# Layer 0 of a two-layer encoder: the attention gate's modulation row summed on TensorE, a different cut of the input projection, and reshaped LayerNorm chains

## The chip, the core and the metric

The kernel runs on one core of a Trainium2 chip. It is given the device time in microseconds (us), the median of three runs. The engines named below are TensorE (PE, with its weight loads shown as PEld), VectorE (DVE), ScalarE (ACT), GpSimd (POOL) and SyncE (SP), which issues all the transfers of this kernel on one queue. TensorE accumulates in PSUM; the other data lie in SBUF. All weights are float32 in HBM, and each is read once.

## The reference, cut to what matters

One sequence of 256 tokens with 2048 features goes through two layers. The modulation of a layer is a product of one row, the SiLU of the condition `c`, with a matrix of 2048 x 12288; it is cut into six parts of 2048 numbers each (shift, scale and gate of the attention block, then of the feed-forward block).

```python
cond = jax.nn.silu(c)
for l in range(DEPTH):
    mod = cond @ w_ada[l] + b_ada[l]
    sh1, sc1, g1, sh2, sc2, g2 = [m[:, None, :] for m in jnp.split(mod, 6, axis=-1)]
    u = x * (1.0 + sc1) + sh1
    proj = u @ w_in[l]
    ...            # three attention groups, their outputs RMS-normalised and joined to y
    x = layer_norm(DEEPNORM_ALPHA * x + (1.0 + g1) * (y @ w_o[l]), ln1_g[l], ln1_b[l])
    u = x * (1.0 + sc2) + sh2
    gu = u @ w_gu[l]
    h = jax.nn.silu(gu[..., :D_FF]) * gu[..., D_FF:]
    x = layer_norm(DEEPNORM_ALPHA * x + (1.0 + g2) * (h @ w_down[l]), ln2_g[l], ln2_b[l])
return x
```

## The kernel before, in words

Activations are held with features on the 128 partitions and the 256 tokens along the free axis; a row of 2048 features is 16 such tiles, numbered k on the input side and n on the output side of a product. Weights arrive as 1 MB transfers of 128 x 2048 (`wload`, L238 to L262). Most are split in two halves of 1024 columns into a rounded part `hi` (ACT, L254) and a rest `lo` (DVE, L255), so that a float32 product is made of three fast matmuls of 256 columns: hi times the rounded input, hi times the input's rest, lo times the rounded input. In `gemm_t` (L283) the first two are one matmul of 512 columns; `mm_one` (L308) issues them as three lines, L310 to L312. Nine of the sixteen `w_o` tiles of layer 0 are not split but multiplied in full float32 (`wload_f32`, `gemm_f32`, L279); a float32 matmul shows in the trace as two instructions.

All 1 MB loads of split weights and of the modulation matrix share four buffers, the tag `raw`. A load is issued by SP when the fourth load before it has been used up, and SP issues in program order.

**Modulation.** `ada` (L199) loads one block of 128 modulation columns (1 MB) and sums it against the condition in one DVE instruction (L207, `ada<-ada,cond,vec`). The order is a list, `ada_pending`: for each k the scale and shift of layer 0 (parts 1 and 0), then the sixteen blocks of its gate (part 2), then parts 4 and 3, and so on. `pace` takes blocks from this list at a fixed number per us of planned work; `need` forces those that are wanted next.

**Layer 0, front.** `first_x` (L433) makes input tile X[k] when its two modulation sums are there. The 14 tiles in `RES` accumulate in PSUM while X arrives, one k at a time (`rows`, `in_r` in the trace). The nine tiles in `ROT` use one PSUM bank in turn (`in_rot`): from k = 8 on, each gets its first 8 k values in one go while X arrives (`first_half`), and its last 8 later, as a filler between attention heads (`w_in_tile`, `in`). `_stream0` (L55) writes the weights in that order.

**Attention.** `weave` (L764) runs a group's heads with a list of fillers, one ahead of each head, and up to three pieces of other work around the group's RMS normalisation (`normed`). The groups are a (4 heads), b (6) and c (6). The value projections `va` and `vc`, the query and key expansions `qn`, `qp`, `kn`, the values `vb` and, in group c, the first ten k values of seven `w_o` tiles (`oh`) are such pieces. In `rms_bcast` (L351) the inverse norms of the tokens are put on a diagonal by two DVE instructions and spread over the partitions by a matmul with ones.

**LayerNorm.** `residual` (L567) adds an output tile into `ax` and keeps two running sums over the tiles, s1 of the values and s2 of the squares (L582, L583). After the last tile, `ln_and_next` (L462) reduces both over the partitions (`token_stat`, `lnst`), works out mean and inverse deviation on columns of two, puts the four columns on diagonals (DVE L481, ACT L483), spreads them by two matmuls (`lnbr`, `lnbn`) and makes the next X tiles. `spin` puts idle matmuls between, so that TensorE does not stand still. The split of the next stage's first weights is held back until the residual of tile KT - 3 = 13 is done (`lastr`, `gates`). L999 has a one-element Sqrt (`warm`) ahead of the third tile of the last feed-forward product.

## Time and profile before

| | us |
|---|---|
| three runs | 2296.77, 2297.22, 2301.22 |
| median | 2297.22 |
| the profiled execution, own time | 2295.78 |
| its span, first to last instruction | 2294.0 |
| TensorE busy in it | 2211.5 (96%) |
| VectorE busy in it | 1732.6 (76%) |
| ScalarE busy in it | 1224.9 (53%) |

The profiled execution is 1.4 us below the median of the runs. Busy time of TensorE is modelled and includes overlap of neighbouring matmuls, so 96% does not say that it ran at its peak; shares over the whole span mix stages with different limits, and the rows further below are therefore taken by stage. The rows of windows name the engines by their place: PE, PEld, DVE, ACT, POOL. In layer 0 the stages follow the program: X arrives until 162 us, the attention groups run until 370 us, the remaining `w_o` tiles until 432.6 us, the first LayerNorm until 439 us, and the feed-forward block until 1181 us; its LayerNorm ends at 1194 us, and layer 1 ends the span.

### The profile page before, as it was taken

To read this page: it belongs to the slowest core of one execution; us is meant where nothing else is said; L and a number is where in the kernel's file an instruction comes from. 1 tells how busy PE (TensorE), PEld (TensorE's weight loads), DVE (VectorE), ACT (ScalarE), POOL (GpSimd) and SP (SyncE) were. 2 spreads that over 40 slices of the span, in tenths; PEclk is the share of its full clock that TensorE was granted. 3 is DMA by queue.
4 is the path that set the end of the run, shared out by engine and by line. 5 is a ranking of instruction groups with operands and counts; after the bars stand their busy time and mean duration, and the time that the engine had idled before them with its cause. 6 is when DMAs were issued, how large, how long until landed. Compare 5 with 4: busy or idle time off the path is not lost.

```text
span 2294.0 us, 33731 instructions
## 1 busy us (share of the span) xinstructions
PE 2211.5 (96%) x13074; PEld 1964.7 (86%) x13074; DVE 1732.6 (76%) x2444; ACT 1224.9 (53%) x2038; POOL 207.2 (9%) x175
## 2 busy tenths in 40 slices
PE   6888999999999999999999999999999999999997
PEld 5787988898888888888878898878888888888886
DVE  6778998688888888898888576788666665566566
ACT  3337672464555455445557566557455545545555
POOL 0000020000000310110230000330000020011014
PEclk9999999999999999999999999999999999999999
DMA  9997899568998798799755554456577566546542
GB/s 355 354 363 289 324 333 366 209 246 303 323 329 328 281 361 335 256 354 338 286 192 215 201 217 165 155 194 236 195 249 265 213 222 228 186 164 212 195 157 105
DMA packets 89730, 590.64 MB, mean 257 GB/s; under 512 B 10081, under 2 KB 10209, under 8 KB 31329
## 3 DMA queue, kind: packets, MB, share of 16 engines
q1 hardware_dynamic: 89570, 588.49, 70.1%
q8 instruction: 102, 1.67, 0.3%
q14 instruction: 58, 0.48, 0.1%
HBM read 586.35 MB, written 2.10 MB: 257 GB/s over the span
## 4 chain that ended last, share of the span: by engine, by line
PE 87%; DVE 7%; ACT 3%; issue 2%; POOL 1%; DMA 0%; ACTq 0%; DVEq 0%
PE gu L288 25%; PE gu L290 13%; PE dn L288 13%; PE dn L290 7%; PE in L288 3%; PE o L279 3%; DVE ada L207 3%; DVE lo L255 2%; PE in L290 1%; ACT hi L254 1%; PE oh L605 1%; PE gu_h L605 1%; PE in L605 1%; PE in_r L310 1%; PE gu L312 1%
## 5 line engine op out<-in xcount | busy, mean ns | idle before, releaser
L255 DVE TENSOR_TENSOR lo<-raw,hi 128x1024 fp32r<-128x1024 f32 (+2 forms) x790 | 878.4, 1139 | 317.2 <-issue 149.2
L254 ACT ACTIVATE hi<-raw 128x1024 fp32r<-128x1024 f32 (+2 forms) x790 | 758.9, 968 | 460.8 <-PE gu L288 193.1
L288 PE MATMUL gu<-X,hi 128*128 128x512 f32 x2528 | 603.1, 391 | 0.0
L288 PEld LDWEIGHTS gu<-X,hi 128*128 128x128 f32 x2528 | 465.1, 188 | 89.5
L207 DVE CUSTOM_DVE_ANT_0 ada<-ada,cond,vec 128x2048 f32<-128x2048 f32 x192 | 450.0, 2351 | 30.0 <-DMA ada<-in_w_ada 20.7
L288 PE MATMUL dn<-H,hi 128*128 128x512 f32 x1386 | 339.7, 392 | 0.2 <-DVE H L337 0.2
L290 PEld LDWEIGHTS gu<-X,lo 128*128 128x128 f32 x2528 | 324.2, 191 | 12.3
L290 PE MATMUL gu<-X,lo 128*128 128x256 f32 x2528 | 328.0, 283 | 0.0
L288 PEld LDWEIGHTS dn<-H,hi 128*128 128x128 f32 x1386 | 252.6, 189 | 49.6 <-DVE H L337 3.0
L290 PEld LDWEIGHTS dn<-H,lo 128*128 128x128 f32 x1386 | 183.1, 191 | 9.9 <-DVE lo L255 0.3
L290 PE MATMUL dn<-H,lo 128*128 128x256 f32 x1386 | 186.5, 283 | 0.1
L332 POOL TENSOR_TENSOR mix<-mix,cma 128x256 f32<-128x256 f32 x64 | 80.7, 1261 | 1148.7 <-ACT cma L331 1116.3
L324 ACT ACTIVATE cmb<-gu 128x256 f32<-128x256 f32 x158 | 60.5, 383 | 114.8 <-PE gu L290 114.7
L310 PE MATMUL in_r<-X,hi 128*128 128x256 f32 x224 | 66.7, 319 | 37.1 <-ACT X L336 34.8
L310 PEld LDWEIGHTS in_r<-X,hi 128*128 128x128 f32 x224 | 47.2, 220 | 41.6 <-ACT X L336 39.0
L983 ACT ACTIVATE gu<-gu 128x256 f32<-128x256 f32 x82 | 34.1, 417 | 81.6 <-DVE gu L327 81.6
L897 POOL TENSOR_SCALAR nbc<-cs 128x384 f32<-128x384 f32 x12 | 24.4, 2030 | 566.6 <-DVE mn_c L397 255.2
L337 DVE TENSOR_TENSOR H<-gu,H 128x256 fp32r<-128x256 f32 x82 | 34.6, 423 | 48.6 <-ACT H L336 48.6
L311 PE MATMUL in_r<-X,hi 128*128 128x256 f32 x224 | 69.4, 315 | 0.1
L288 PE MATMUL in<-X,hi 128*128 128x512 f32 x272 | 69.5, 402 | 0.0
L327 DVE SCALAR_TENSOR_TENSOR gu<-gu,cmb 128x256 f32<-128x256 f32 x158 | 66.3, 419 | 1.0 <-ACT cmb L324 0.4
L312 PE MATMUL in_r<-X,lo 128*128 128x256 f32 x224 | 66.4, 309 | 0.4 <-DVE lo L255 0.4
(385 smaller groups left out, 3043.0 us busy)
## 6 DMA issues: line engine op xcount, KB each, us to landing
ada<-in_w_ada SPq DMA_DIRECT2D x192, 1024.0 KB, 5.4
raw<-in_w_gu SPq DMA_DIRECT2D x176, 1024.0 KB, 5.2
raw<-in_w_dn SPq DMA_DIRECT2D x128, 704.0 KB, 4.1
raw<-in_w_in SPq DMA_DIRECT2D x46, 1024.0 KB, 5.3
raw<-in_w_o SPq DMA_DIRECT2D x23, 1024.0 KB, 4.8
wf<-in_w_o SPq DMA_DIRECT2D x18, 512.0 KB, 10.3
raw<-in_w_va SPq DMA_DIRECT2D x8, 1024.0 KB, 4.8
raw<-in_w_uq SPq DMA_DIRECT2D x6, 1024.0 KB, 4.9
```

What stands on the lines that cost most here:

```text
L207: ve.tensor_tensor_reduce(out=w, in0=w, in1=cond, op0=ALU.mult, op1=ALU.add, scale=1.0, scalar=vcol(l, V_ADA + part * KT + k), accum_out=m ...
L254: ac.activation(out=hi[:, :n], in_=raw[:, c0:c0 + n], func=AF.Copy)
L255: eng.tensor_tensor(out=lo[:, :n], in0=raw[:, c0:c0 + n], in1=hi[:, :n].bitcast(F32), op=ALU.subtract)
L279: m_ = pe.matmul(acc[:, :S], lhsT=w[i // 8][:, i % 8 * P:(i % 8 + 1) * P], rhs=X[k][:], start=(i == 0), stop=(i == len(kts) - 1))
L288: pe.matmul(acc[:], lhsT=get(c0 + i * P, P)[0], rhs=X[kts[i]][:], start=(i == 0), stop=False)
L290: last_mm[0] = raw_ins(pe.matmul(acc[:, :S], lhsT=get(c0 + i * P, P)[1], rhs=X[kts[i]][:, :S], start=False, stop=(i == n - 1)))
L310: m_ = pe.matmul(acc[:, :S], lhsT=h, rhs=x[:, :S], start=first, stop=False, **kw)
L311: pe.matmul(acc[:, :S], lhsT=h, rhs=x[:, S:], start=False, stop=False, **kw)
L312: last_mm[0] = raw_ins(pe.matmul(acc[:, :S], lhsT=lo, rhs=x[:, :S], start=False, stop=end, **kw))
L327: ve.scalar_tensor_tensor(out=dst, in0=acc[:, :S], scalar=scale, in1=t, op0=ALU.mult, op1=ALU.add)
L332: po.tensor_tensor(out=dst, in0=dst, in1=t, op=ALU.add)
L605: pe.matmul(acc[:], lhsT=h, rhs=x[:], start=first, stop=False)
```

## The change

**Gate on TensorE.** The sixteen gate blocks of layer 0 (part 2, `PE_ADA`) are no longer summed by DVE. `ada_pe` loads a block of the matrix in the other orientation (input features on the partitions) and runs 16 float32 matmuls over it, each with one column of the condition repeated over 32 columns as weights and 128 columns of the block as moving data. Matmul i writes the PSUM strip of 32 partitions that begins at 32 * (i % 4) (`tile_position`), so four partial sums are left. ACT copies them out (128 x 128), and at the next load `fold_rows` adds the four strips with one matmul against a column `sel` that has a one at every 32nd partition; ACT adds the bias.

**Input tiles.** The nine `ROT` tiles go to k = 12 while X arrives, in two pieces of 6 k values, at the places that `_rows` lists; the last 4 follow as fillers. The fillers of layer 0's groups a and b are dealt out anew.

**`w_o` tiles.** Of the nine float32 tiles of layer 0, the even ones (8, 10, 12, 14) are split and multiplied by `gemm_one`.

**LayerNorm.** The sums of tiles 0 to 14 are reduced by `ln_sums` ahead of the last four k values of tile 15's product; tile 15's own values and squares are reduced straight from `ax` and the square, without going through s1 and s2. The diagonals are gone: each column is repeated over 128 columns as weights of a matmul with the identity, here and in `rms_bcast`. Of the idle matmuls, the first six go, six become four, and seven become five. Tile 14's additions move from POOL to DVE, and the next stage's first splits wait for tile 14 in place of 13. The one-element Sqrt is tied to the last SiLU.

```diff
+KP = 6
+def _rows():
+    todo = [(j, c) for c in range(2) for j in range(len(ROT))]
+    per = {6: 2, 7: 2, 8: 2, 9: 2, 10: 1, 12: 2, 13: 2, 14: 2, 15: 3}
+    return [(k, [todo.pop(0) for _ in range(per.get(k, 0))]) for k in range(KT)]
...
+PE_ADA = ((0, 2),)
...
+            if (l, part) in PE_ADA:
+                ada_pe(l, part, k)
+                continue
...
+    def ada_pe(l, part, k):
+        fold_rows()
+        w = wp.tile([P, D], F32, tag="raw", bufs=RAWB, name=f"adap{l}_{part}_{k}")
+        sy.dma_start(out=w, in_=w_adag[PE_ADA.index((l, part)), k])
+        acc = pg(f"arow{l}_{part}_{k}")
+        first = None
+        for i in range(KT):
+            j = 32 * (i % 4)
+            with after(first):
+                m_ = pe.matmul(acc[j:j + 32, :P], lhsT=condT[:, i:i + 1].to_broadcast([P, 32]),
+                               rhs=w[:, i * P:(i + 1) * P], start=(i < 4), stop=(i >= KT - 4), tile_position=(0, j))
+            first = first or raw_ins(m_)
+        r = sb.tile([P, P], F32, tag="arow", bufs=2, name=f"arsb{l}_{part}_{k}")
+        ac.activation(out=r, in_=acc[:, :P], func=AF.Copy)
+        folds.append((l, part, k, acc, r))
+
+    def fold_rows():
+        while folds:
+            l, part, k, acc, r = folds.pop(0)
+            pe.matmul(acc[:, S:S + 1], lhsT=r[:], rhs=sel, start=True, stop=True)
+            ac.activation(out=mods[l, part][:, k:k + 1], in_=acc[:, S:S + 1], func=AF.Identity,
+                          bias=vcol(l, V_ADA + part * KT + k), scale=1.0)
...
-        dg = tmp(f"dg_{name}", "dg", 2)
-        for h in range(2):
-            ve.tensor_scalar(out=dg[:, h * P:(h + 1) * P], in0=ident, scalar1=r[:, h:h + 1], scalar2=None,
-                             op0=ALU.mult)
...
-        pe.matmul(bc[:, :S], lhsT=ones, rhs=dg[:], start=True, stop=True)
+        for h in range(2):
+            pe.matmul(bc[:, h * P:(h + 1) * P], lhsT=r[:, h:h + 1].to_broadcast([P, P]), rhs=ident, start=True, stop=True)
...
-        st = pa("y", 1, f"lnst{l}_{which}")
-        spin(f"a{l}_{which}", 6)
-        token_stat([s1, s2], inv[2048], [0, 2], st)
-        spin(f"b{l}_{which}", 6)
+        ln_sums(l, which, [(ax[:, KT - 1], last_sq)], False, True)
+        st = stat[0]
+        spin(f"b{l}_{which}", 4)
...
-            if i < 2:
-                ve.tensor_scalar(out=d_, in0=ident, scalar1=m[:, i:i + 1], scalar2=None, op0=ALU.mult)
-            else:
-                ac.activation(out=d_, in_=ident, func=AF.Copy, scale=m[:, i:i + 1])
...
+            last_mm[0] = raw_ins(pe.matmul((bcr if i < 2 else bcn)[:, i % 2 * P:(i % 2 + 1) * P],
+                                           lhsT=m[:, i:i + 1].to_broadcast([P, P]), rhs=ident, start=True, stop=True))
...
-            po.tensor_tensor(out=ax[:, n], in0=ax[:, n], in1=t, op=ALU.add)
+            (ve if final and n == KT - 2 else po).tensor_tensor(out=ax[:, n], in0=ax[:, n], in1=t, op=ALU.add)
...
+                if n == KT - 1:
+                    return q
...
-                if l == 0:
-                    gemm_f32(acc, wload_f32(w_o[l, n]), Yf, allk)
+                if l == 0 and n % 2:
+                    gemm_f32(acc, wload_f32(w_o[l, n]), Yf, allk, sums_in if n == KT - 1 else None)
...
+                    if l == 0:
+                        gemm_one(acc, get, 0, Y, allk)
...
-            if n == KT - 3:
+            if n == KT - 2:
                 lastr = r_
...
-                    ac.activation(out=warm, in_=eps_ln, func=AF.Sqrt)
+                    with after(silu[0]):
+                        ac.activation(out=warm, in_=eps_ln, func=AF.Sqrt)
```

What this does to the order of the instructions is shown at three places. The first is PE in layer 0, behind the last `in_rot` matmuls. `st_kv` is the first RMS sum, `in_22` the filler tile 22, `va` the value projection of group a, and in the names of the changed kernel `adap` is a gate block, `arow` its strips and `arsb` their copy. Before, tile 22 has 24 matmuls left there (three of them are shown), then the projection begins:

```order
L344 MATMUL st_kv_1493<-inv_109,sqk_139 128x1 x2
L310 MATMUL in_22_8_1466<-X_8_699,hi_1_1404 128x256
L311 MATMUL in_22_8_1466<-X_8_699,hi_1_1404 128x256
L312 MATMUL in_22_8_1466<-X_8_699,lo_1_1405 128x256
...
L428 MATMUL s_a_0_1701<-ka_0_119,qa_0_115 128x256 x2
L428 MATMUL s_a_1_1784<-ka_1_120,qa_1_116 128x256
L669 MATMUL va_0_1502<-hi_0_1509,X_0_160 128x512
L669 MATMUL va_1_1503<-hi_0_1509,X_0_160 128x512
```

In the changed kernel the same place reads:

```order
L362 MATMUL in_22_12_1627<-X_15_1451,hi_1_1552 128x256
L363 MATMUL in_22_12_1627<-X_15_1451,hi_1_1552 128x256
L364 MATMUL in_22_12_1627<-X_15_1451,lo_1_1553 128x256
L396 MATMUL st_kv_1642<-inv_112,sqk_142 128x1 x2
L252 MATMUL arow_2_0_1527<-cs,arsb_2_0_1544 128x1
L241 MATMUL arow_2_1_1654<-adap_2_1_1652,condT 32x128 x16
L730 MATMUL va_0_1648<-hi_0_1675,X_0_163 128x512
L730 MATMUL va_1_1649<-hi_0_1675,X_0_163 128x512
```

Tile 22 is finished ahead of `st_kv` with 12 matmuls, and a gate block's fold and the next block's 16 matmuls stand ahead of the projection; thirteen of the sixteen gate blocks stand on PE between X[15] and the first scores of group b, six of them (1 to 6) from here to the end of `va`.

The second place is SP's queue behind the last modulation pair of X, before:

```order
L205 DMA ada_1_15_1344<-in_w_ada 128x2048
L205 DMA ada_0_15_1348<-in_w_ada 128x2048
L246 DMA raw_1398<-in_w_in 128x2048
L155 DMA cs<-in_consts 128x1024
L156 DMA snk<-in_sink 128x12
L752 DMA nba_123<-in_rpb 128x1536
L205 DMA ada_2_0_1504<-in_w_ada 128x2048
L246 DMA raw_1507<-in_w_va 128x2048
```

and in the changed kernel:

```order
L294 DMA raw_1394<-in_w_in 128x2048
L221 DMA ada_1_15_1442<-in_w_ada 128x2048
L221 DMA ada_0_15_1446<-in_w_ada 128x2048
L294 DMA raw_1466<-in_w_in 128x2048
L235 DMA adap_2_0_1525<-in_w_adag 128x2048
L294 DMA raw_1546<-in_w_in 128x2048
L167 DMA cs<-in_consts 128x1025
L168 DMA snk<-in_sink 128x12
```

One more `w_in` load stands ahead of the pair (19 in place of 18), and two `w_in` loads with the first gate block between them stand behind it, where one was.

The third place is DVE at the end of layer 0's feed-forward block, before:

```order
L574 SCALAR_TENSOR_TENSOR ax<-dn_3_13_11149,mod_5_100,ax 128x256
L583 TENSOR_TENSOR s_0_2_10590<-s_0_2_10590,rq_dn_3_13_11176 128x256
L255 TENSOR_TENSOR lo_0_11353<-raw_11350,hi_0_11352 128x1024
L255 TENSOR_TENSOR lo_1_11357<-raw_11350,hi_1_11356 128x1024
L574 SCALAR_TENSOR_TENSOR ax<-dn_3_14_11190,mod_5_100,ax 128x256
L583 TENSOR_TENSOR s_0_2_10590<-s_0_2_10590,rq_dn_3_14_11217 128x256
L569 SCALAR_TENSOR_TENSOR ax<-dn_3_15_11231,mod_5_100,ax 128x256
L582 TENSOR_TENSOR s_0_2_10589<-s_0_2_10589,ax 128x256
L583 TENSOR_TENSOR s_0_2_10590<-s_0_2_10590,rq_dn_3_15_11266 128x256
L470 TENSOR_TENSOR lnm_2_11289<-lnst_2_11270,lnm_2_11289 128x2
```

and in the changed kernel:

```order
L632 TENSOR_TENSOR ax<-ax,rt_dn_3_14_11675 128x256
L633 SCALAR_TENSOR_TENSOR ax<-dn_3_14_11652,mod_5_103,ax 128x256
L643 TENSOR_TENSOR s_0_2_11048<-s_0_2_11048,ax 128x256
L644 TENSOR_TENSOR s_0_2_11049<-s_0_2_11049,rq_dn_3_14_11679 128x256
L303 TENSOR_TENSOR lo_0_11803<-raw_11800,hi_0_11802 128x1024
L303 TENSOR_TENSOR lo_1_11807<-raw_11800,hi_1_11806 128x1024
L628 SCALAR_TENSOR_TENSOR ax<-dn_3_15_11693,mod_5_103,ax 128x256
L536 TENSOR_TENSOR lnm_2_11744<-lnst_2_11715,lnm_2_11744 128x2
```

The two splits for layer 1 moved behind tile 14's additions but still stand ahead of tile 15's, and the two additions into the sums behind tile 15 are gone. On ACT, before, the table load for Sqrt stands between the square of the mean (L469) and the Sqrt itself (L471); in the changed kernel it stands with the one-element Sqrt, some 70 instructions earlier.

## Rows read from the trace of the kernel before

**Rows 1.** Windows by stage: length, busy us (instructions) per engine, PEclk, DMA share, GB/s.

```profile
0.00:162.00 162.00, 121.92 (x830) 112.99 (x830) 121.70 (x122) 61.28 (x101) 0.19 (x4) 0.93 0.92 354
162.00:182.40 20.40, 16.75 (x95) 16.46 (x96) 9.51 (x12) 12.85 (x28) 2.58 (x2) 0.69 0.69 269
182.40:207.50 25.10, 25.10 (x114) 20.70 (x114) 25.06 (x43) 14.01 (x25) 0.00 (x0) 1.00 0.81 301
207.50:249.60 42.10, 37.88 (x253) 34.80 (x253) 37.85 (x63) 26.61 (x59) 0.00 (x0) 0.96 0.84 311
249.60:307.30 57.70, 55.12 (x381) 50.56 (x379) 55.80 (x92) 41.69 (x92) 1.17 (x1) 1.00 0.90 339
307.30:370.50 63.20, 58.87 (x425) 55.20 (x426) 62.01 (x112) 39.23 (x86) 14.00 (x5) 0.97 0.88 327
370.50:432.60 62.10, 62.10 (x289) 54.80 (x288) 38.88 (x65) 7.20 (x16) 0.00 (x0) 1.00 0.88 356
1181.40:1194.00 12.60, 9.58 (x34) 7.05 (x32) 6.63 (x18) 4.78 (x10) 2.31 (x2) 0.73 0.31 121
```

**Rows 2.** Waits of the DMA queue, 155 to 400 us: total, times, longest.

```profile
SPq L205 <- DVE mod L207: 51.3, 18, 6.5
```

**Rows 3.** X's scaling (first and last start us), and transfers from 0 to 150 us.

```profile
L437 ACT ACTIVATE u<-ax,mod,mod x16: 589/599/601, 15.0 to 160.9; 128x256 f32<-128x256 f32 x16
DMA packets 7719, 53.37 MB, mean 356 GB/s; under 512 B 849, under 2 KB 977, under 8 KB 1489
```

**Rows 4.** DVE by form, 162 to 249.6 us, then 249.6 to 370.5 us: busy, mean ns.

```profile
L207 DVE CUSTOM_DVE_ANT_0 ada<-ada,cond,vec 128x2048 f32<-128x2048 f32 x15 | 35.1, 2347 | 1.3 <-DMA ada<-in_w_ada 1.3
...
L207 DVE CUSTOM_DVE_ANT_0 ada<-ada,cond,vec 128x2048 f32<-128x2048 f32 x25 | 58.8, 2357 | 0.0
L255 DVE TENSOR_TENSOR lo<-raw,hi 128x1024 fp32r<-128x1024 f32 x26 | 31.1, 1221 | 2.3 <-ACT hi L254 2.1
```

**Rows 5.** Chain of waits: start, us, what (x instructions, one after another).

```profile
188.13 0.23 PE va L669
370.46 62.16 PE o L279 x288
1520.98 5.76 PE o L300 x48
```

**Rows 6.** Timeline, short matmuls and weight loads: start, us.

```profile
219.48 0.60 PE L417 MATMUL ptp_a<-cs,pp_a 128*128 128x128 f32 x4
220.03 0.28 PE L310 MATMUL in<-X,hi 128*128 128x256 f32 x1
220.15 0.28 PE L311 MATMUL in<-X,hi 128*128 128x256 f32 x1
2276.28 0.54 PEld L344 LDWEIGHTS lnst<-inv,s 128*128 128x128 f32 x4
```

**Rows 7.** Timeline, layer 0's last LayerNorm: DVE, then ACT.

```profile
1184.91 0.47 DVE L569 SCALAR_TENSOR_TENSOR ax<-dn,mod,ax 128x256 f32<-128x256 f32 x1
1191.74 0.42 DVE L534 TENSOR_TENSOR lt<-ax,lnbr 128x256 f32<-128x256 f32 x1 [1.31 <-PE lnbr L485]
...
1188.05 1.28 ACT L471 ACT_TABLE_LOAD   x1
```

**Rows 8.** Timeline, the final LayerNorm: PE, then DVE, in order of time.

```profile
2276.40 0.95 PE L344 MATMUL lnst<-inv,s 128*128 128x1 f32 x8
2277.21 1.63 PE L459 MATMUL spinb<-H 128*128 128x512 f32 x6
2280.00 0.70 PE L485 MATMUL lnbr<-lndg,cs 128*128 128x256 f32 x2 [1.16 <-DVE lndg L481]
...
2276.24 0.43 DVE L583 TENSOR_TENSOR s<-s,rq_dn 128x256 f32<-128x256 f32 x1
2279.20 0.17 DVE L472 RECIPROCAL lnm<-lnm 128x2 f32<-128x2 f32 x1 [1.45 <-ACT lnm L471]
```

More of the change, by code (lines that the diff above doesn't have):

```diff
@@ L150, in tile_encoder @@
     sy.dma_start(out=vec, in_=vecs)
+    condT = cst.tile([P, KT], F32, name="condT")
+    sy.dma_start(out=condT, in_=cT)
     snk = cst.tile([P, L * C_HEADS], F32, name="snk")
@@ L299, in gemm_last @@
         for i, (w, x) in enumerate(ops):
+            if between and i == len(ops) - 12:
+                between()
             m_ = pe.matmul(acc[:, :S], lhsT=w, rhs=x, start=(i == 0), stop=(i == len(ops) - 1))
@@ L459, in spin, with ln_sums, ln_and_next @@
                 pe.matmul(d_[:], lhsT=live[0][:, :P], rhs=live[0][:], start=True, stop=True)
-    def ln_and_next(l, which, s1, s2, last, q1, a1):
+    stat = {}
+    def ln_sums(l, which, pairs, first, end):
+        if first:
+            stat[0] = pa("y", 1, f"lnst{l}_{which}")
+        for j, pair in enumerate(pairs):
+            for c in range(4):
+                with after(opened_[0] if first and j == 0 and c else None):
+                    m_ = raw_ins(pe.matmul(stat[0][:, c:c + 1], lhsT=pair[c // 2][:, c % 2 * P:(c % 2 + 1) * P],
+                                           rhs=inv[2048], start=first and j == 0 and c == 0,
+                                           stop=end and j == len(pairs) - 1, skip_group_check=True))
+                if first and j == 0 and c == 0:
+                    opened_[0] = m_
+        last_mm[0] = m_
+    opened_ = [None]
+    def ln_and_next(l, which, last_sq, last, q1, a1):
         gb = V_LN1G if which == 1 else V_LN2G
-        st = pa("y", 1, f"lnst{l}_{which}")
-        spin(f"a{l}_{which}", 6)
-        token_stat([s1, s2], inv[2048], [0, 2], st)
-        spin(f"b{l}_{which}", 6)
+        ln_sums(l, which, [(ax[:, KT - 1], last_sq)], False, True)
+        st = stat[0]
+        spin(f"b{l}_{which}", 4)
         m = sb.tile([P, 8], F32, tag="lnsm", bufs=2, name=f"lnm{l}_{which}")
@@ L474, in ln_and_next @@
                                 op0=ALU.mult, op1=ALU.mult)
-        dg = sb.tile([P, 512], F32, tag="pts", bufs=2, name=f"lndg{l}_{which}")
         bcr = pa("pt", 1, f"lnbr{l}_{which}")
@@ L637, in w_in_tile @@
             if l == 0:
[L638 removed]
+                take_add(st_in.tile(n, 2 * KP, KT), dst, scale)
                 return
@@ L732, in rows, with piece_of @@
                     opened = st_in.mm(res[n], n, k, k == 0, k == KT - 1, **kw)
-            def first_half(j):
+            turn = [0]
+            def piece_of(j, c):
                 n = ROT[j]
-                half = rot[:, j % 2 * S:(j % 2 + 1) * S]
-                take(st_in.tile(n, 0, HK, half), dst[n][0], dst[n][1])
-            for k in range(HK):
+                half = rot[:, turn[0] % 2 * S:(turn[0] % 2 + 1) * S]
+                turn[0] += 1
+                st_in.tile(n, c * KP, c * KP + KP, half)
+                (take_add if c else take)(half, dst[n][0], dst[n][1])
+            for k, pieces in _rows():
                 x_of(k)
                 rows(k)
-            for j in range(HK):
-                first_half(j)
-                x_of(HK + j)
-                rows(HK + j)
-            first_half(HK)
-            credit[1] = RATE[l][0]
+                if k == KT - 1:
+                    credit[1] = RATE[l][0]
+                for j, c in pieces:
+                    piece_of(j, c)
             for n in RES[8:] + RES[:8]:
```

80 lines of the change are left out of this document (50 added, 30 removed).

## The prediction

> **What bounds the kernel now.** I read the windows by stage first, since shares over the whole span mix stages with different limits [rows 1]. Up to 162 us the DMA share is 0.92 at 354 GB/s, while TensorE and VectorE have 40 and 49 us to spare; an X tile comes every (160.9 - 15.0) / 15 = 9.7 us on average, in the order in which its loads land [rows 3]. This stage is bound by transfers. At 356 GB/s [rows 3] one load of 1 MB (1.049 million bytes) takes 2.95 us. From 162 to 182.4 us nothing is full: the granted clock is 0.69 and the stage runs off what X left over. From 182.4 to 207.5 us TensorE is busy for 25.10 of 25.10 us and VectorE for 25.06: two engines are full at once. From there to 370.5 us VectorE is the fullest (37.85 of 42.1, 55.80 of 57.7, 62.01 of 63.2 us), with TensorE and the transfers close behind; that VectorE leads is seen again at the queue, which waits 51.3 us, 18 times, for a block of the modulation to be summed before it may load the next [rows 2]. From 370.5 to 432.6 us TensorE is full (62.10 of 62.10) with VectorE at 38.88 us. So an edit that moves work from VectorE to TensorE can pay between 207 and 370 us alone, and must cost between 182 and 207 us.
>
> **Front.** In the order one more 1 MB load stands ahead of the last pair, so X[15] comes 2.95 us later, near 164; one more small transfer at the start (the condition, turned) I put at 0.4 us. After X[15] TensorE had 16.75 us of work in 20.4 us at a low clock. In the changed order 42 row matmuls, 54 of the last three pieces, 12 of tile 22 and the first gate block stand there: 108 x 0.12 (one begins 0.12 us behind the other [rows 6]) = 13 us, plus 1 us for the block, plus some 3 us for the low clock that the stage showed. That ends at 165 + 17 = 182 to 183, where the projection began before. I take +0.6 us with the small transfer; the idle time of before is the cover, and without it the 2.95 us would show whole.
>
> **One gate block on TensorE.** It is 16 float32 matmuls of 128 columns. The trace shows a float32 matmul as two instructions, and `ptp`, with the same 128 columns, has four instructions begin within 0.60 us, the last needing its own run through [rows 6]; I read 0.108 us between starts from (0.60 - 0.28) / 3. One after another that is 32 x 0.108 = 3.46 us, the upper bound. If four strips of 32 columns run side by side, it is a quarter, 0.86 us, the lower bound. The fold is one float32 matmul with one column, 2 instructions of (0.95 / 8) = 0.12 us [rows 8], 0.24 us. No row of before shows strips. I take 1.2 us a block, near the low end, because the sixteen matmuls write four disjoint parts of one bank and weights are loaded while other matmuls run: the loads for four `lnst` matmuls, 0.54 us from 2276.28, run on under those matmuls, which begin at 2276.40 [rows 6, 8].
>
> Here a rule speaks against it. The load row shows loads of the same 128 rows under a running matmul [rows 6]. The Trainium skill, page "TensorE: Matmul & The Clock Gate", section "Part 3: Packing small matmuls — row/col tiling", says that a weight load overlaps matmuls in flight only when its row group differs; here all sixteen use all rows, and only the column strip differs. By that rule the block would be serial, which is rival C. The same section gives 2.38 times for three column strips, which no run here shows; 3.46 / 2.38 = 1.45 us would be an estimate from it.
>
> Thirteen blocks stand ahead of the first scores of group b and three behind. **182 to 207 us:** TensorE is full, six blocks add 6 x 1.2 = +7.2 us. **207 to 250 us:** four fillers have 4 k values left in place of 8, so 4 x 4 x 3 x 0.12 = 5.8 us leave TensorE and six blocks put 7.2 back: 37.9 - 5.8 + 7.2 = 39.3 us. VectorE, which held 37.85, sums no block at all up to the scores of group b, where it summed fifteen of 2.35 us from 162 us on [rows 4], and is no bound any more. The stage is then as long as TensorE's work and what TensorE still waits for at the heads, of which I keep 1.2 of the 4.2 us that it stood idle before: 40.5 for 42.1, -1.6 us. So group b begins 0.6 + 7.2 - 1.6 = 6.2 us later.
>
> **Groups b and c, 249.6 to 370.5 us.** VectorE has 117.8 us of 120.9. The order has 23 modulation blocks and 20 splits of 1024 there in place of 25 and 26: 2 x 2.36 + 6 x 1.22 = 12.0 us go [rows 4], and the diagonals about 1. It falls to 105. TensorE has 55.12 + 58.87 = 114.0 us, less 5.8 for four more halved fillers, plus 3.6 for three blocks: 112. Its busy time there counts neighbours' overlap, so I put it at 109 to 112. The transfers had 0.90 x 57.7 + 0.88 x 63.2 = 107.5 us, and lose one or two loads. No engine would be as far ahead as VectorE was, and three engines with 105 to 112 us of work that wait for each other are not done in 112: I take 114, a gain of 7 us; the bounds are 0 and 10. The first full `w_o` tile then begins 0.8 us earlier than at 370.46 [rows 5].
>
> **`w_o` tiles.** Nine take 62.16 us, 6.91 each [rows 5]. A split tile of 48 matmuls took 5.76 us in layer 1 [rows 5]. Four change: 4 x 1.15 = -4.6 us. VectorE gets eight splits of 1.22 us on 38.88 (about 10 us), and the transfers 18 MB x 2.95 = 53 us of 57.5: neither takes over, though the transfers are close.
>
> **LayerNorm chains.** In the final one the second sum's addition (0.43 us, from 2276.24) goes; the broadcast ended at 2280.70, and would, from the reciprocal's end at 2279.37 plus 0.06 for a wait, 0.43 for two matmuls and 0.17 for the small product, end at 2280.03: 0.67 us [rows 8]. Behind a feed-forward block the table load, 1.28 us [rows 7], goes too. Against it stand eight small matmuls put into tile 15's product: 2276.40 to 2277.21 is 0.81 us for eight [rows 8]. Final: 0.43 + 0.67 + 1.28 - 0.81 = -1.6 us. The two first LayerNorms: 0.43 + 0.67 - 0.81, -0.3 each. Layer 0's second one: the order of VectorE (two splits still ahead of tile 15) sets tile 15's addition at 1184.91 [rows 7], so the eight are covered there: -2.4; its 12.6 us ran at 0.73 of the clock [rows 1], 3.4 us' worth lost, of which I let a shorter gap give back 0.9: -3.3. Sum -5.5 us; zero to -8 are the bounds. Where tile 14's additions run on VectorE instead of POOL, they are hidden by tile 15's product, and a wait for tile 14 in place of 13 costs only if that product is shorter than the splits (2 x 1.22 us), which it isn't. The diagonals in the RMS normalisations are covered by the piece that runs between them on TensorE: 0.
>
> **Sum.** 6.2 - 7 - 4.6 - 5.5 = -10.9 us on the profiled 2295.78: 2284.9. That execution lies 1.4 us below the median, so the forecast is 2286 us.
>
> **Rivals.** All but the last turn on the price of one block. The terms for it are thirteen blocks ahead of group b, and each 0.1 us a block costs 1.3 us; the gain of 10.9 is used up at 1.2 + 0.84 = 2.0 us.
> B: strips overlap, but only by half: 3.46 / 2 + 0.24 = 2.0 us, about 2.05 us a block with a little for the change between whole and strip matmuls. That is +0.85 x 13 = +11: 2297 us, no change. For it: every block is surrounded by ordinary matmuls, so thirteen blocks bring 26 changes of shape. By the Trainium skill, page "TensorEngine Tiling (Array Packing)", on mode switching, a change of the tiling mode drains TensorE; it gives no figure, and no row here shows one.
> C, slower: strips run one after another, 3.46 + 0.24 = 3.7 us. +2.5 x 13 = +32, and three blocks in groups b and c take 5 of the gain there, since TensorE then has 7.5 us more to do: 2286 + 37 = 2323 us. It decides from 2.4 us a block on, where the forecast's gain is used up and 0.2% lost. Against it: four disjoint strips have nothing to wait for in each other.
> D: VectorE's relief reaches its bound and groups b and c take 107 us, the transfers' time: 7 us more, 2279 us.
> E: the change doesn't do what it says in the LayerNorms, because the shorter idle matmuls let the clock fall where it held: 5.5 us less gain, 2291 us; this lies within the forecast's own range. The order shows the table load moved, which speaks for the chains.
>
> **How the numbers follow.** Forecast with E: 0.60, its own range 2280 to 2292. B: 0.20. C: 0.15. D: 0.05. A measurement can tell about 0.2% of this kernel, 4.6 us, so faster means below 2292.6 and slower above 2301.8. Faster: nearly all of the forecast and D, and a little of B: 0.65. Same: most of B and the forecast's edge: 0.17. Slower: C and B's upper end: 0.18. The range leaves out C (0.15) and some 0.03 below: it goes from 2275, where D's term meets the best LayerNorm case, to 2303, the far end of B (2.5 us a block).
>
> **What would show it.** In the profile after: the group of `arow` at 1 us a block (3.5 us says C); no sum of modulation on VectorE between X[15] and the first scores of group b, where 35 us were; TensorE full from X[15]'s rows to the first scores of group b, which come near 256; the first full `w_o` tile near 369.7 and the nine in 57 to 58 us; no table load in the LayerNorms behind the feed-forward blocks, and in layer 0's the first `lt` about 3 us sooner behind tile 15's addition than 1191.74 - 1184.91 = 6.8 us. X[15] after 166 would make the front wrong, an o stage of 62 us the fourth term, a first `w_o` tile past 375 the whole forecast.

## The result and the profile after

The changed kernel takes 2309.99 us (median of six runs, 2307.78 to 2314.53) against 2296.99 us of the kernel before: a ratio of 1.0053, 95% interval 1.0043 to 1.0064. It is slower by 0.5%, where 2286 us and a range of 2275 to 2303 us had been forecast. The profiled execution has a span of 2306.0 us, 12.0 us more than before.

The windows by stage of the changed kernel (length, then busy us and instructions of PE, PEld, DVE, ACT, POOL, then granted clock, DMA share, GB/s) answer to [rows 1]:

```profile
164.00:184.90 20.90, 18.77 (x200) 17.72 (x198) 10.70 (x20) 15.05 (x32) 2.34 (x2) 1.00 0.85 327
184.90:215.40 30.50, 30.50 (x258) 25.43 (x254) 14.44 (x28) 14.37 (x30) 0.00 (x0) 1.00 0.74 281
215.40:252.70 37.30, 37.30 (x437) 33.76 (x435) 16.05 (x36) 27.43 (x70) 0.00 (x0) 1.00 0.80 303
252.70:308.20 55.50, 55.50 (x464) 51.39 (x462) 46.11 (x75) 38.96 (x91) 0.00 (x0) 1.00 0.87 330
308.20:373.00 64.80, 57.71 (x415) 53.72 (x414) 62.76 (x122) 41.62 (x94) 15.13 (x6) 0.97 0.83 312
373.00:445.00 72.00, 61.21 (x362) 55.57 (x360) 50.63 (x76) 15.76 (x26) 0.00 (x0) 0.93 0.82 315
```

TensorE is now full from 184.9 to 308.2 us, while VectorE has fallen to half and less until 252.7. In group c (308 to 373) VectorE is as full as before. And the last row is the surprise: the stage of the full `w_o` tiles, which was 62.1 us long with TensorE full, takes 72.0 us with a clock of 0.93.

Followed along the program, the loss builds up like this (starts read off the timelines): X[15] +3.8, first value matmul +1.5, first full `w_o` tile +2.7 (373.0 for 370.3), end of the last `w_o` tile +12.4, first matmul of the feed-forward block +11.1, start of the last product's stage in layer 0 +13.3, first matmul of layer 1 +11.8, feed-forward block of layer 1 +13.4, end +12.0. So 9.7 of the 12 us arise in one stage.

TensorE in that stage (timeline, idle time in brackets with what ended it):

```profile
381.07 0.67 PE L329 MATMUL o<-yra,wf 128*128 128x256 f32 x2 [0.78 <-DVE mod L223]
382.51 0.38 PE L364 MATMUL o<-Ya,lo 128*128 128x256 f32 x1 [0.78 <-DVE lo L303]
414.52 0.58 PE L362 MATMUL o<-Ya,hi 128*128 128x256 f32 x1 [7.10 <-ACT hi L302]
417.45 0.58 PE L364 MATMUL o<-Ya,lo 128*128 128x256 f32 x1 [2.14 <-DVE lo L303]
```

Tile 12 is where it stands still. The queue of SP tells why. Its timeline in the changed kernel (first and last issue of a run of loads):

```profile
389.10 15.47 SPq L221 DMA_DIRECT2D ada<-in_w_ada  x5
406.51 4.51 SPq L294 DMA_DIRECT2D raw<-in_w_o  x2
411.12 0.86 SPq L321 DMA_DIRECT2D wf<-in_w_o  x2
```

and in the kernel before, at the same place:

```profile
381.64 13.66 SPq L205 DMA_DIRECT2D ada<-in_w_ada  x4
395.39 9.96 SPq L273 DMA_DIRECT2D wf<-in_w_o  x8
405.45 5.94 SPq L246 DMA_DIRECT2D raw<-in_w_gu  x4
```

The program wants the modulation of the feed-forward block complete before it turns to tile 12 (`need` at n = KT - 4), and forces what is left of it into the queue there: five blocks now, four before. Behind them stood `wf` loads, which do not share the four `raw` buffers; now tile 12's load wants one of these. It is issued 11.1 us later than before (406.5 for 395.4), and 9.3 us of that are the blocks: their run ends at 404.6 in place of 395.3 (start and length of the two rows added). The other 1.9 us are the wait for a `raw` buffer, until an earlier block has been summed. Before, the first half of tile 12's load landed 8.8 us behind its issue, at 404.2, and tile 12 began at 404.8: it came just in time. Now it lands 5.9 us behind its issue, at 412.4, while TensorE stands still from 407.4 on. ScalarE's timeline has the rest:

```profile
413.31 0.21 ACT L210 ACTIVATE mod<-mod 128x4 f32<-128x4 f32 x1 [4.92 <-DVE mod L223]
413.42 1.99 ACT L302 ACTIVATE hi<-raw 128x1024 fp32r<-128x1024 f32 x2
```

The split of tile 12 stands in program order behind the end of the last forced group of blocks, and that waits for VectorE's sum; this is 1.0 of the 7.1 us.

### The profile page after: what moved, and what is told of

The parts are those of the page before. It is cut to its first block, busy times and chain, and to the rows that moved or that the text cites. A ratio compares the mean times of both kernels' runs of the same rounds, so it can differ in the third digit from the quotient of the medians.

```text
span 2306.0 us, 34990 instructions
## 1 busy us (share of the span) xinstructions
PE 2217.4 (96%) x13710; PEld 1969.9 (85%) x13710; DVE 1705.0 (74%) x2399; ACT 1233.3 (53%) x2070; POOL 197.3 (9%) x169
## 4 chain that ended last, share of the span: by engine, by line
PE 84%; DVE 9%; ACT 3%; issue 2%; DMA 1%; POOL 1%; ACTq 0%; DVEq 0%; SPq 0%
PE gu L338 25%; PE gu L340 13%; PE dn L338 11%; PE dn L340 6%; DVE ada L223 3%; DVE lo L303 3%; PE in L338 3%; PE in L340 1%; PE o L329 1%; ACT hi L302 1%; PE oh L666 1%; DMA ada<-in_w_ada 1%; PE gu_h L666 1%; PE in L666 1%; PE arow L241 1%
## 5 line engine op out<-in xcount | busy, mean ns | idle before, releaser
L303 DVE TENSOR_TENSOR lo<-raw,hi 128x1024 fp32r<-128x1024 f32 (+2 forms) x798 | 888.0, 1141 | 317.9 <-issue 137.4
L302 ACT ACTIVATE hi<-raw 128x1024 fp32r<-128x1024 f32 (+2 forms) x798 | 766.6, 969 | 468.9 <-PE gu L338 191.0
L223 DVE CUSTOM_DVE_ANT_0 ada<-ada,cond,vec 128x2048 f32<-128x2048 f32 x176 | 413.6, 2357 | 45.4 <-DMA ada<-in_w_ada 36.2
L340 PEld LDWEIGHTS gu<-X,lo 128*128 128x128 f32 x2528 | 324.1, 191 | 13.3 <-DVE lo L303 1.0
L384 POOL TENSOR_TENSOR mix<-mix,cma 128x256 f32<-128x256 f32 x64 | 75.4, 1178 | 1165.8 <-ACT cma L383 1131.2
L362 PE MATMUL in_r<-X,hi 128*128 128x256 f32 x224 | 64.4, 305 | 31.0 <-ACT X L388 22.1
L363 PE MATMUL in_r<-X,hi 128*128 128x256 f32 x224 | 66.1, 301 | 0.1
```

The lines of the kernel that those rows point to most:

```text
L223: ve.tensor_tensor_reduce(out=w, in0=w, in1=cond, op0=ALU.mult, op1=ALU.add, scale=1.0, scalar=vcol(l, V_ADA + part * KT + k), accum_out=m ...
L302: ac.activation(out=hi[:, :n], in_=raw[:, c0:c0 + n], func=AF.Copy)
L303: eng.tensor_tensor(out=lo[:, :n], in0=raw[:, c0:c0 + n], in1=hi[:, :n].bitcast(F32), op=ALU.subtract)
L340: last_mm[0] = raw_ins(pe.matmul(acc[:, :S], lhsT=get(c0 + i * P, P)[1], rhs=X[kts[i]][:, :S], start=False, stop=(i == n - 1)))
L362: m_ = pe.matmul(acc[:, :S], lhsT=h, rhs=x[:, :S], start=first, stop=False, **kw)
L363: pe.matmul(acc[:, :S], lhsT=h, rhs=x[:, S:], start=False, stop=False, **kw)
```

## The experiments

Medians, ratios and intervals are against the runs of the kernel before on the same chip (whose medians lay between 2295.4 and 2297.8 us). The last three columns are read off the timelines of the profiled executions, in us: start of the first full `w_o` tile, length of that stage, first matmul of the feed-forward block.

| run | median | ratio, 95% interval | w_o | stage | next |
|---|---|---|---|---|---|
| before | | 1 | 370.3 | 62.3 | 439.0 |
| changed | 2309.99 | 1.0053, 1.0043 to 1.0064 | 373.0 | 72.1 | 450.1 |
| before_o_split | 2306.80 | 1.0045, 1.0031 to 1.0059 | 369.4 | 70.5 | 446.2 |
| o_full | 2306.10 | 1.0038, 1.0024 to 1.0053 | 372.7 | 69.3 | 447.0 |
| o_early | 2310.26 | 1.0057, 1.0042 to 1.0072 | 373.1 | 73.2 | 451.3 |
| ada_sooner | 2317.21 | 1.0089, 1.0074 to 1.0104 | 383.2 | 68.4 | 456.6 |
| five_blocks_less | 2298.74 | 1.0008, 0.9998 to 1.0019 | 374.9 | 60.6 | 440.5 |
| before_four_less | 2296.93 | 1.0003, 0.9993 to 1.0012 | 372.3 | 62.3 | 440.9 |
| blocks_behind | 2300.29 | 1.0013, 1.0003 to 1.0022 | 374.0 | 65.4 | 444.4 |
| gate_on_dve | 2307.45 | 1.0044, 1.0030 to 1.0058 | 370.0 | 72.5 | 447.6 |
| gate_alone | 2312.32 | 1.0064, 1.0050 to 1.0079 | 385.9 | 62.3 | 454.5 |
| rows_alone | 2303.70 | 1.0037, 1.0023 to 1.0051 | 365.5 | 69.5 | 441.3 |
| rows_blocks_behind | 2296.94 | 1.0007, 0.9999 to 1.0016 | 366.7 | 62.3 | 435.3 |
| ln_alone | 2294.13 | 0.9983, 0.9974 to 0.9993 | 371.0 | 63.2 | 439.2 |
| ln_split_behind | 2295.95 | 0.9998, 0.9988 to 1.0008 | 372.6 | 63.8 | 441.4 |
| ln_rows_behind | 2293.24 | 0.9990, 0.9981 to 1.0000 | 368.1 | 63.2 | 436.4 |

### Is it the split of the w_o tiles?

The part alone, on the kernel before:

```diff
-                if l == 0:
+                if l == 0 and n % 2:
                     gemm_f32(acc, wload_f32(w_o[l, n]), Yf, allk)
...
+                    if l == 0:
+                        gemm_one(acc, get, 0, Y, allk)
```

> The kernel before with this one part of the change: w_o tiles 8, 10, 12 and 14 of layer 0 split and multiplied in three fast matmuls. Four forced blocks stand ahead of tile 12 here. Theory A: the stage is 66 to 72 us against 62.2, and the whole 2301 to 2307 us, with the longest wait of TensorE at tile 12. Rival: the loss needs the other parts of the change (a later queue); then the stage is near 57.6 us and the whole near 2292.

It costs 0.45% by itself, and the wait sits at tile 12, as theory A has it. Its timeline of TensorE:

```profile
410.03 0.58 PE L310 MATMUL o<-Ya,hi 128*128 128x256 f32 x1 [4.49 <-ACT hi L254]
412.97 0.58 PE L312 MATMUL o<-Ya,lo 128*128 128x256 f32 x1 [2.14 <-DVE lo L255]
```

Taken back in the changed kernel:

```diff
-                if l == 0 and n % 2:
+                if l == 0:
```

> The changed kernel with all nine full tiles of w_o in layer 0 multiplied in float32 again, as before. Theory A: the split tiles share the four raw buffers with modulation blocks, and the split of tile 12 waits behind five blocks that are forced ahead of it; then the w_o stage, 72.1 us in the changed kernel, falls to nine times 6.91 plus 0.8 us for the sums, 63 us, no idle time of TensorE over 1 us in it, and the whole to 2299 to 2303 us. Theory B: the stage is late for what groups b and c leave behind (a queue that comes out of them later); then it stays at 69 us or more and the whole near 2308.

Theory A falls short here, and the numbers are those of theory B. Without any split tile the stage is still 69.3 us long, and only 4 of the 13 us of the whole are won back. The wait is at the same tile, but a transfer ends it:

```profile
411.49 2.87 PE L329 MATMUL o<-yra,wf 128*128 128x256 f32 x8 [4.12 <-DMA wf<-in_w_o]
```

So tile 12's load itself comes late in the changed kernel, in whichever form: here, without a `raw` buffer, it is issued at 404.7, right behind the blocks. Two attempts to get around the forced blocks, first with other tiles split, then with the blocks loaded sooner:

```diff
-                if l == 0 and n % 2:
+                if l == 0 and n > 10:
```

> The changed kernel, but the tiles that are split and multiplied in three fast matmuls are 7, 8, 9 and 10, ahead of the forced modulation blocks, and 11 to 15 are float32. Theory A: the stage takes 4 x 5.76 + 5 x 6.91 + 0.8 = 58.4 us, with no wait of 7 us at tile 12, and the whole is 2295 to 2298 us. Rival: four more loads in the shared buffers are too many for the stage wherever they stand; then TensorE stands still for as long among tiles 7 to 11 and the stage is 66 us or more, the whole over 2303.

```diff
-RATE = ((0.24, 0.135, 0.135), (0.04, 0.05, 0.05))
+RATE = ((0.27, 0.135, 0.135), (0.04, 0.05, 0.05))
```

> The changed kernel with the modulation paced at 0.27 blocks per planned us in layer 0's attention in place of 0.24, so that one block and not five is forced ahead of tile 12 of w_o; the tiles split are 8, 10, 12 and 14, as in the changed kernel. Theory A: the stage takes 58 to 61 us, and as VectorE has room in the attention groups since the gate left it, the first full tile begins no more than 3 us later; the whole 2296 to 2301. Rival (too many loads in the shared buffers): the stage stays over 66 us, the whole over 2305.

Both went the way of the rival. With tiles 7 to 10 split, TensorE waits 5.4 us at the second of them and 4.0 at tile 12. With the blocks sooner, the first full `w_o` tile comes 10 us later, presumably since they go ahead of loads that the attention groups wait for (this was not tested by itself); 2.6 of the 10 are not theirs, as X[15] came at 167.3 in this execution with the same loads ahead of it (164.7 to 166.1 in most others of this cut, 167.3 in one more).

### Is it the transfers?

From here theory C is tested: the loads in the queue ahead of tile 12 came just in time before, so that nothing in this stage could get shorter, and anything that holds the queue up shows there. Five blocks, or four, are replaced by a constant:

```diff
             l, part, k = ada_pending.pop(0)
+            if skip[0]:
+                ve.memset(mods[l, part][:, k:k + 1], 0.5)
...
+                skip[0] = l == 0
                 need(l, 3, KT - 1 if l else KT - 1 - DEFER // 2)
+                skip[0] = False
```

> The changed kernel without the five modulation blocks of layer 0 (parts 4 and 3) that are forced ahead of w_o tile 12: they are neither loaded nor summed, a constant stands in their place, so this part of the computation is left out. 5 MB less ride in the queue. Theory C (the w_o stage is bound by the transfers that stand in the queue ahead of tile 12, and the loads had no time to spare before): the stage falls from 72.1 to 58 to 60 us with no wait of TensorE over 1 us at tile 12, and the whole to 2295 to 2298. Rival (the split tiles themselves, by the order of VectorE and ScalarE, hold TensorE up): waits of 2 us or more stay at tiles 8 to 14, and the whole stays over 2303.

> The kernel before without its four forced blocks (parts 4 and 3 of layer 0, neither loaded nor summed, a constant in their place: this part is left out). 4 MB less in the queue. Theory C: TensorE had no wait in that stage before, the loads came just in time; so nothing is gained, the stage stays at 62 to 62.5 us, the whole within 2 us of 2296.7, and only the landing of tile 12's load moves, some 10 us earlier. Rival: transfers held the stage before as well; then it gets shorter by 2 us or more.

Both came out as theory C has it (the first one's stage 0.6 us and its whole 0.7 us above their brackets). The stage of the changed kernel, from its own first to last full tile:

```profile
374.80:435.50 60.70, 59.15 (x362) 54.12 (x360) 39.31 (x67) 15.82 (x27) 0.00 (x0) 1.00 0.76 288
```

TensorE runs at full clock with 1.5 us of waits, none of them at tile 12. On the kernel before, the saving of 4 MB bought nothing: TensorE had no wait there to lose. That the loads were a second bound there, of the same length up to tile 12, is seen in the kernel before from 376 to 414 us, where TensorE is busy for 38.00 of 38.00 us and the DMA engines are full too (share 1.02, 415 GB/s):

```profile
376.00:414.00 38.00, 38.00 (x178) 33.54 (x177) 28.35 (x40) 2.71 (x7) 0.00 (x0) 1.00 1.02 415
```

With nothing left out, the blocks are dealt out behind tiles 12, 13 and 14:

```diff
             if n == KT - 4:
-                need(l, 3, KT - 1 if l else KT - 1 - DEFER // 2)
+                if l:
+                    need(l, 3, KT - 1)
                 credit[1] = 0.0
...
+            if l == 0 and n >= KT - 4:
+                for _ in range(2):
+                    if (l, 3, KT - 1) in ada_pending:
+                        ada(1)
             r_ = residual(l, acc, n, mods[l, 2][:, n:n + 1], s1, s2, True, f"o{l}_{n}", l == 0)
```

> The changed kernel with nothing left out, but the five modulation blocks that were forced ahead of w_o tile 12 are dealt out behind the loads of tiles 12 (two), 13 (two) and 14 (one). Theory C1 (what holds TensorE is the place of these loads in the one queue): tile 12's wait of 7.1 us goes, the w_o stage takes 59 to 62 us and the whole 2297 to 2301. Theory C2 (the sum of the transfers in the stage, 22 MB, sets its length, wherever each stands): the wait moves to tile 13 or 14 or to the LayerNorm, the stage and the LayerNorm together stay over 72 us, the whole over 2305.

It lies between the two: 9.7 us less than the changed kernel in the whole, yet a stage of 65.4 us. The window and the waits of TensorE left:

```profile
374.00:439.40 65.40, 61.13 (x362) 55.55 (x360) 50.44 (x77) 15.54 (x26) 0.00 (x0) 0.97 0.90 344
```

```profile
423.06 0.38 PE L362 MATMUL o<-Ya,hi 128*128 128x256 f32 x1 [1.97 <-ACT hi L302]
424.33 0.38 PE L364 MATMUL o<-Ya,lo 128*128 128x256 f32 x1 [0.76 <-DVE lo L303]
```

Most of the loss was the place of the loads (C1). Of the 4.3 us of waits that remain, 0.6 end with a load and the rest with a split. They are not the sum of the transfers (C2), as the longest one shows: tile 14's load landed at 416.2 (issued at 408.1, 8.1 us to landing), TensorE had done tile 13 at 421.1, and yet it waited 2.0 us for the split. ScalarE's timeline:

```profile
420.19 0.21 ACT L210 ACTIVATE mod<-mod 128x4 f32<-128x4 f32 x1 [5.04 <-DVE mod L223]
421.65 0.42 ACT L640 ACTIVATE rq_o<-ax 128x256 f32<-128x256 f32 x1 [1.25 <-DVE ax L628]
421.97 1.99 ACT L302 ACTIVATE hi<-raw 128x1024 fp32r<-128x1024 f32 x2
```

It first waits for VectorE's sum of a block and for the square of tile 13, which needs the end of that tile, and splits right behind them. So what remains comes with the split tiles themselves, by the order of ScalarE and VectorE, as the rival named for five_blocks_less has it. The same order of the loads on a kernel without split tiles and without the gate on TensorE settles the first half; it uses the new cut of the input tiles, which is shown alone first (its diff is the change's `_rows`, `_stream0`, `piece_of` and the two `weave` calls):

> The kernel before with the new cut of the input tiles (twelve k values while X arrives, in two pieces) and the fillers of groups a and b dealt out anew, and nothing else. The forecast put X[15] 3 us later and the first value matmul less than 1 us later, and 5.8 us of filler work out of each of the next two stretches, which VectorE's sums bound here. Theory C: the loads that the fillers no longer need were taken before X[15], their sum is unchanged; the first full w_o tile stands within 2 us of 370.3, the whole within 3 us of 2296.7. Rival: VectorE and TensorE both get room and the first w_o tile comes 4 us sooner, the whole at 2293 or less.

> The kernel before with the new cut of the input tiles and fillers, and with the modulation blocks that were forced ahead of w_o tile 12 dealt out behind tiles 12 to 14; nothing else. Theory C1 (place in the queue): the wait of 4.1 us that the cut alone had at tile 12 goes, the w_o stage takes 62 to 63 us from 365.5, and the LayerNorm ends near 434.5; the whole is 2292 to 2299, at least 4 us under the cut alone (2303.7). Theory C2 (sum of transfers): the wait moves to tiles 13 to 15 or the LayerNorm; the head of the feed-forward block still begins at 440 or later and the whole stays within 3 us of 2303.7.

The cut alone brings the first full `w_o` tile 4.9 us sooner, more than theory C allowed, and is slower by 0.37% all the same; neither bracket of the whole had that. Five blocks are forced there, and tile 12's load landed at 404.1, just when it had landed before, although the stage began 4.9 us sooner. The first matmul of the feed-forward block comes 2.3 us later than before; the profiled span is 5.9 us longer, and where the rest arises was not followed. Its one wait in the stage, and the stage of the run with the blocks behind:

```profile
404.22 3.75 PE L286 MATMUL o<-yra,wf 128*128 128x256 f32 x8 [4.08 <-DMA wf<-in_w_o]
```

```profile
366.60:429.00 62.40, 62.40 (x291) 54.96 (x291) 41.76 (x69) 8.34 (x20) 0.00 (x0) 1.00 0.91 362
```

With the five loads behind tile 12, its load landed at 398.0 (384.2 + 13.8), 3.2 us ahead of its tile, TensorE is full again, and the feed-forward block begins at 435.3, 3.7 us sooner than before and 6 sooner than with the cut alone. So it is the place in the queue. But the whole is only even with the kernel before: 2 us of the 3.7 are gone by the first down product. The longest wait there, 1.8 us at 443.8 us for an X tile that ScalarE makes, explains little of it, since the kernel before has one of 1.25 us for the same; what costs the rest was not found.

### What the gate on TensorE costs

Summed by VectorE again, all else as changed (`if (l, part) in PE_ADA` made false):

> The changed kernel with the sixteen gate blocks summed by VectorE again; all else as changed. Theory C: the loads in layer 0's attention come at a pace that the summing engine hardly sets, so the first full w_o tile begins within 3 us of 373, the stage after it stays near 72 us with its wait at tile 12, and the whole is 2307 to 2313. Rival: TensorE was full from 185 to 308 us with the sixteen blocks, so taking 13 x 1.2 us from it brings the first w_o tile to 366 or earlier and the whole to 2303 or less.

And the gate alone on the kernel before:

> The kernel before with the gate blocks of layer 0 on TensorE, and the diagonals of the RMS normalisation gone (their room in SBUF is needed); input tiles, fillers, w_o tiles and LayerNorms as before. By the trace of the changed kernel a block costs TensorE 1.2 us and TensorE was full from 182 to 207 us and 90% busy from there to 250, so the first scores of group b come 6 to 12 us later; groups b and c give back what VectorE no longer has to do, until the transfers bound them. Theory C (the loads are the bound of layer 0 up to its LayerNorm and had no time to spare): the first full w_o tile begins 0 to 4 us later than at 370.3 and each us of that shows at tile 12 again; the whole 2297 to 2302. The forecast's sum for these parts: -1 us at the first w_o tile, the whole near 2296.

The first agrees with theory C: 2.5 us in the whole, the first `w_o` tile 3.0 us sooner. The second missed both brackets: 385.9 us, 15.6 us later than before. Its windows around groups a and b, and what its queue waits for from 160 to 310 us (total, times, longest):

```profile
184.00:215.00 31.00, 31.00 (x260) 25.21 (x252) 15.67 (x24) 13.50 (x27) 0.00 (x0) 1.00 0.78 275
252.00:305.00 53.00, 53.00 (x472) 49.41 (x471) 40.07 (x64) 33.39 (x83) 0.00 (x0) 1.00 0.87 324
```

```profile
SPq L228 <- PE arow L234: 44.4, 8, 17.5
SPq L287 <- PE arow L234: 19.1, 6, 6.2
```

TensorE had been the second full engine, busy for 90 to 100% of each stage from 182 to 370 us [rows 1]; sixteen blocks of 1.2 us are 19 us more for it, less what it stood idle, and VectorE's relief buys nothing. In addition the queue now waits for TensorE: a gate block keeps its buffer until its matmuls come up in TensorE's order. What this wait costs by itself was not tested. In the changed kernel the same row stands from 164 to 373 us, where [rows 2] had VectorE:

```profile
SPq L294 <- PE arow L241: 33.6, 8, 6.6
SPq L235 <- PE arow L241: 22.5, 6, 5.9
```

With the new cut the gate costs far less at the first `w_o` tile: 3.0 us (373.0 for 370.0 with the blocks on VectorE). An estimate says why: the eight fillers behind the first value matmul have 4 k values less, 8 x 4 x 3 x 0.12 = 11.5 us off TensorE, and 15.6 - 11.5 = 4.1.

### What the LayerNorm chains gain

> The kernel before with the reshaped LayerNorm chains alone (sums of tiles 0 to 14 ahead of the end of tile 15, no diagonals, fewer idle matmuls, tile 14's additions on VectorE, splits behind tile 14, the one-element Sqrt tied to the last SiLU). The forecast's own sum for it was -5.5 us: 2291. What the trace of the changed kernel shows at the four chains adds to -3 to -4 us: 2293. Rival: the later splits of the next stage's first weights and tile 14's additions cost as much elsewhere as the chains save; then 2295 to 2298.

Between the forecast's sum and the rival: 0.17% faster, 2.4 us by the medians (the profiled execution, with a span 4.6 us shorter, lies 2.9 us below its median). It is the one part that pays alone. With the split tiles and the blocks behind:

> The kernel before with the LayerNorm part of the change, with tiles 8, 10, 12 and 14 of w_o split, and with the forced modulation blocks dealt out behind the loads of tiles 12 to 14; no gate block on TensorE, the input tiles cut as before. Theory C1: the w_o stage takes 58 to 60 us against 62.2, and the whole is 2289 to 2292, under the LayerNorm part alone (2294.1). Theory C2: the stage is 62 us or more again, or the first w_gu splits come that much later, and the whole is 2294 or more.

The split gains nothing even so: the stage is 63.8 us and the whole over 2294, the numbers of theory C2. Its reason is not borne out: TensorE is busy for 59.4 of the 63.8 us, and its three waits, 4.4 us in all, end with splits of ScalarE and VectorE, the longest again at tile 14, whose load had landed at 415.2, 6 us before TensorE could begin it. And with the new cut in their place:

> The same with the LayerNorm part of the change added. If the gains add up: 2.4 us less than the run beside it, and under 2294 if theory C1 holds there. Rival: the eight small matmuls and the later splits take the room that is left; no less than the run beside it.

The two add up, 3.7 us under the run beside it; against the kernel before it is no better than the LayerNorm part alone (0.9990 and 0.9983, intervals that overlap). Only the LayerNorm part alone is faster than the kernel before beyond its interval, by little; the interval of this one reaches 1.0000.

## Why the prediction was wrong, step by step

**The step that failed is the `w_o` stage.** It was forecast 4.6 us shorter and came 9.7 us longer, 14.3 of the 24 us by which the forecast missed. The step is "the transfers 18 MB x 2.95 = 53 us of 57.5: neither takes over". Its size was wrong by the row in front of it: 356 GB/s over 62.1 us [rows 1] are 22.1 million bytes, 21 loads, since modulation blocks and the next stage's weights ride in it too. But the path was wrong above all. A sum over the stage does not see the order: what counts is what stands in the queue ahead of tile 12. Up to there transfers and TensorE had been full together (376 to 414 us, above), and tile 12's load landed 0.6 us before its tile began, so whatever got shorter by more in front of it turned into a wait. As a sum over the stage the transfers were no bound: at those 415 GB/s the 21 loads are an estimated 53 us, the run with the cut and the blocks behind brings the loads in time, and the changed kernel, with 315 GB/s, is far from full. The changed stage is 4 x 5.76 + 5 x 6.91 + 0.8 = 58.4 us of work, 10.8 us of waits (the four rows of TensorE above), and nearly 2 us at the low clock: the 17 matmuls behind the long wait mostly start 0.21 us apart in place of 0.12, at a granted clock of 0.50; some 1 us was not told apart:

```profile
407.40:414.50 7.10, 0.02 (x1) 0.00 (x0) 6.74 (x10) 1.60 (x4) 0.00 (x0) 0.70 0.89 332
414.50:420.60 6.10, 3.94 (x17) 3.65 (x18) 5.13 (x6) 1.97 (x2) 0.00 (x0) 0.50 1.02 387
420.60:424.40 3.80, 3.80 (x33) 3.80 (x33) 1.23 (x1) 1.06 (x1) 0.00 (x0) 1.00 0.61 252
```

**The price of a gate block was right**, on which rivals B and C turned. The timeline of TensorE at block 2:

```profile
191.76 0.28 PE L252 MATMUL arow<-cs,arsb 128*128 128x1 f32 x2
191.97 1.08 PE L241 MATMUL arow<-adap,condT 128*32 128x128 f32 x32
192.98 0.50 PE L730 MATMUL va<-hi,X 128*128 128x512 f32 x1
```

From 191.76 to 192.98 are 1.22 us, for the fold and the block, where 1.2 were taken; 1.01 of them are the block, and the matmul behind it starts with no wait. So the loads overlapped: 32 of 0.105 us, 3.4 us, went by within the 1.01, all on the same 128 rows. The Trainium skill, page "TensorE: Matmul & The Clock Gate", section "Part 3: Packing small matmuls — row/col tiling", lets a weight load overlap matmuls in flight only where its row group differs; this trace disagrees. Nor did the changes of shape decide: the next matmul starts 0.20 us behind the start of the block's last one, within the 1.22. The Trainium skill, page "TensorEngine Tiling (Array Packing)", section "Key Properties", says that a change of the tiling mode drains TensorE; whatever a drain costs here is contained in the 1.22 us. The tile's own summary (duration in ns as least, median, most):

```profile
L241 PEld LDWEIGHTS arow<-adap,condT x512: 105/110/110, 177.6 to 265.2; 128*32 128x32 f32 x171
```

Rival C, the slower side, was therefore the wrong mechanism with the right sign. No rival had the transfers ahead of tile 12 as the cause.

**The front was right in kind**: X[15] at +3.8 (3.35 forecast), the first value matmul at +1.5 (+0.6), the end of the value projection at +7.9 (+7.8).

**Groups a to c** were forecast at -0.8 us at the first `w_o` tile and came at +2.7. The parts were wrong in a way that nearly cancels, which is luck. The forecast let VectorE's relief give 7 us. The run with the gate alone shows that it gives none, with TensorE as full; what the groups did get back came from the new cut (-4.9 alone). The gate takes 3.0 us back, and the 4.6 us between the cut alone (365.5) and the changed kernel with its gate on VectorE (370.0) belong to other parts and were not told apart. Group c stayed bound by VectorE (62.76 of 64.80 us): 12 blocks and 14 splits of 1024 were summed and made there, 13 and 15 before (over groups b and c together 22 blocks and 23 splits, where the forecast had counted 23 and 20).

**The LayerNorm chains** were right where they could be read. From tile 15's addition to the first `lt` layer 0's last one took 6.83 us before [rows 7]; after:

```profile
1199.36 0.48 DVE L628 SCALAR_TENSOR_TENSOR ax<-dn,mod,ax 128x256 f32<-128x256 f32 x1
1203.09 0.42 DVE L593 TENSOR_TENSOR lt<-ax,lnbr 128x256 f32<-128x256 f32 x1 [0.95 <-PE lnbr L544]
```

That is 3.73, 3.1 less, where 3 had been named, and no table load is in it. The stretch from the feed-forward block of layer 1 to the end is 1.4 us shorter (1.6 forecast). But the four chains together show -2 us in place of -5.5 in the changed kernel: tile 15 of layer 0 came 1.2 us later in its product, and the `w_o` stage of layer 1 with its LayerNorm took 1.3 us more in place of 0.3 less. Some 2 us more went in the feed-forward block of layer 0, where TensorE waits twice for 0.6 us for a split. With the LayerNorm part alone the same places show -3.6, -0.2 and +0.5. What in the full change costs these 5 us was not told apart and stays open.

## What to carry to other kernels

Before an engine's work in a stage is cut, count the bytes that the stage moves from its own GB/s and length, and look at what stands in the queue ahead of the tile that comes next: where a load lands as its tile begins, nothing is gained by a faster engine. Two engines at 90% and more are two bounds: moving work from one to the other moves the bound, and the queue then waits for the buffers that the second engine frees in its own order. Gains of single parts don't add: four parts at +14.7, +8.5, +10.3 and -3.9 us (ratios of gate, cut, split and LayerNorms alone) made +12 together. That they used the same few us of slack is an argument, not shown.

## What the runs showed of the hardware that was not expected

That the 16 float32 matmuls of a block, 32 instructions with weights of 32 columns and a weight load each, took 1.01 us: 0.03 us from one start to the next, 0.20 us from the last start to that of the next matmul of the full shape. That the transfers of the kernel before ran at 415 GB/s for 38 us (376 to 414), where their mean over the first 150 us was 356 [rows 3]. And that the granted clock was 0.70 over the wait of 7.1 us and 0.50 (1.2 GHz) in the 6.1 us behind it, at a cost of nearly 2 us on top of the wait.
